# The first stage of a two-layer hybrid backbone: TensorE's order written by hand, fold weights a step ahead, the context moved behind the latent tokens

## The chip, the cores and the metric

The kernel runs on one NeuronCore of a Trainium2 chip. The core has a matrix engine (TensorE, PE in the profile, with its weight loads as PEld), a vector engine (VectorE, DVE), a scalar engine (ScalarE, ACT), GpSimd (POOL) and a queue that issues the loads and stores (SyncE, SP). They run side by side, each in its own fixed order of instructions, and wait for each other through semaphores. The metric is the time of one execution on the device in microseconds (us). Matrix products read SBUF and write PSUM, which has eight banks of 128 x 512 fp32 numbers.

## The reference

The model has two layers. Layer 0 joins a convolution branch and a gated linear recurrence, layer 1 is a pooling mixer. The work of the stage that is changed comes from these lines (cut):

```python
shift, scale, gate = jnp.split(sc @ mod_w[l] + mod_b[l], 3, axis=-1)      # sc = silu(c), 1024 numbers
hx = modulate(rmsnorm(x, norm_g[l]), shift[:, None], scale[:, None])      # x: 1024 tokens x 1024
shift_c, scale_c, gate_c = jnp.split(scc @ mod_w[l] + mod_b[l], 3, axis=-1)
hc = modulate(rmsnorm(ctx, norm_g[l]), shift_c, scale_c)                  # ctx: 256 tokens x 1024
# layer 0
va, vg, ga, xb, gb = jnp.split(hx @ w_in, ...)        # convolution value, its gate, gate A, recurrence input, gate B
xb_c = hc @ w_in[:, 3 * W_CONV:3 * W_CONV + W_LRU]    # the context gives the recurrence its start
u = va * sigmoid(vg)                                  # then a convolution of 31 taps
u_b = depthwise_conv(xb, sconv_w, sconv_b, (2, 1))    # 4 taps, context and latent tokens
r, i = sigmoid(u_b @ w_r + b_r), sigmoid(u_b @ w_i + b_i)      # per head of 128, both directions
log_a = -8 * r * softplus(-lam)                       # "decay rates"
# layer 1
z = h @ w_in;  d = pool(u) - u;  y = einsum(d, w_grp) * scale
```

Pooling acts along the tokens and the group product along the channels, so layer 1's `w_in` and `w_grp` can be multiplied with each other beforehand. The kernel does that ("fold"): 4 groups, each a product of 1024 x 512 by 512 x 512. The output is the latent stream after both layers and a final RMSNorm, in fp32.

## The kernel before

**Layout.** All matrices lie transposed: 128 channels on the partitions, tokens along the row. `x` is 8 tiles of 128 x 1024, the context 8 pieces of 128 x 256 in two tiles of 128 x 1024. Large products keep fp32 accuracy by splitting each operand into a high part (rounded to fp32r) and a low part (the rest), and adding three products: high x high, high x low, low x high. The split is a cast on ScalarE (`split`, L103) and a subtraction (L104) on VectorE or GpSimd. A product of one weight column block with all 8 tiles is 24 matmuls per 512 tokens (`mm3`, `mm3_fixed`).

**The first stage** (from the start to the last `modulate_ctx`). It does three things interleaved by hand in program order:

- *Folds of groups 0 and 1* (`fold`, a generator that `fold_some(n)` advances). One step (g, kp) loads a weight tile `wu`, splits it, and makes two halves s = 0, 1, each 12 matmuls into one PSUM bank (L260 to L262), a copy by ScalarE (L265) and a store to DRAM (`wfold`, L266). The group's own matrix (`graw`, split to `gh`, `gl`) is loaded once.
- *RMSNorm statistics and modulation of the latent tokens.* `x_load(k)` loads a tile and adds its squares (ScalarE squares, VectorE adds). `rstd_cols` turns the sums into roots: small products `ms_x` (L203, one column each), a square root, a diagonal matrix `dg`, and a product of it with ones that spreads the roots over all partitions (L210). The modulation's rows are made in four blocks b: `mod_loads` loads four tiles `modw` of 512 KB, each multiplied with SiLU of c and c_ctx (`modr`, L326, weights of 32 columns); `mod_cols` turns the rows into columns (`modt`, L335). `modulate(k)` then scales tile k, and splits it into `h0h`, `h0l`. A block serves two tiles.
- *The context*: `ctx_load`, `ctx_scale` (root through `ms_c`, L191), `ctx_split`, into `cth`, `ctl`.

**After it** comes a loop over 8 heads j, with every engine's order written by hand (`on` gives each instruction an edge to the one before it on its engine; L444). Step j makes vg, va, the next head's xb and its context part xbc, and the gate products g (L444 all); VectorE makes the recurrence's short convolution (`uc`), the scans and the long convolution, which `fill(n)` hands out tap by tap. In step 0 the gates of layer 0 (the third part of the modulation, for c alone) are made by VectorE: eight tiles of `modT` in the recurrence's tiles `l`, each multiplied with the spread SiLU(c) (`cL`) and summed.

**What sets the order.** In the first stage loads go through `load` (L113), which chains them on SP's queue; stores of the folds are outside of the chain. TensorE's order there is left to a scheduler that orders instructions by its own timeline. At most eight transfers are outstanding: each waits for the one eight places ahead. A pool hands out a tile only when the readers of the one that held its place are done: the weight pool has two places each for raw, high and low parts, the PSUM pool `pm` four banks, `dpool` 16 tiles, `xpool` 8.

Of the kernel before, what the change touches and what calls it, by code (L numbers as in the profile page):

```python
# [15 lines left out]
P = 128  # L16
S = 1024
C = 256
# [38 lines left out]
def body(ctx, tc, xT, ctxT, cc, ccol, modT, modW, win, gw, wout, wu, grp, wg, wo1, small, edge, ident, outT):  # L57
# [49 lines left out]
    chain = [None]  # L107

    def load(out, src):
        with ExitStack() as lctx:  # L110
            if chain[0] is not None:
                lctx.enter_context(tc.issue_after(chain[0].ins))
            d = nc.sync.dma_start(out, src)  # L113
            if chain[0] is not None:
                chain[0] = d

# [28 lines left out]
    nc.sync.dma_start(sm, small)  # L145
    eg = base.tile([P, 4 * 16], F32, name="eg")
    nc.sync.dma_start(eg, edge)
# [23 lines left out]
    nc.scalar.activation(sa, lam, AF.Abs)  # L171
    nc.scalar.activation(sa, sa, AF.Exp, scale=-1.0)
    nc.vector.tensor_scalar(out=sb, in0=sa, scalar1=2.0, scalar2=None, op0=add)
    nc.vector.reciprocal(sb, sb)
    nc.vector.tensor_tensor(out=sz, in0=sa, in1=sb, op=mult)
    nc.vector.tensor_tensor(out=sb, in0=sz, in1=sz, op=mult)
    nc.vector.memset(sa, 1.0 / 17.0)
    for n in range(7, -1, -1):
        nc.vector.tensor_tensor(out=sa, in0=sa, in1=sb, op=mult)
        nc.vector.tensor_scalar(out=sa, in0=sa, scalar1=1.0 / (2 * n + 1), scalar2=None, op0=add)  # L180
    nc.vector.tensor_tensor(out=sa, in0=sa, in1=sz, op=mult)
    nc.vector.tensor_scalar(out=sb, in0=lam, scalar1=-1.0, scalar2=0.0, op0=mult, op1=ALU.max)
    nc.vector.scalar_tensor_tensor(out=sa, in0=sa, scalar=2.0, in1=sb, op0=mult, op1=add)
    nc.vector.tensor_scalar(out=chalf, in0=sa, scalar1=4.0, scalar2=None, op0=mult)
    nc.vector.tensor_scalar(out=cneg, in0=sa, scalar1=-8.0, scalar2=None, op0=mult)
# [11 lines left out]
    def rstd_cols(acc, name, idD, rpool, wn):  # L197
# [4 lines left out]
        for c in range(nt):  # L202
            nc.tensor.matmul(ps[:, c : c + 1], acc[:, c * P : (c + 1) * P], ones[:, 0:1], start=True, stop=True)  # L203
# [6 lines left out]
        nc.tensor.matmul(root[:, :n], ones, t, start=True, stop=True)  # L210
        return root[:, :n]
# [26 lines left out]
    def fold(g, raw_tile, out_tile, g_tile=None, w_tile=None):  # L238
        g_tile = g_tile or dtile
        gh, gl = [], []  # L240
        for i in range(2):
            raw = raw_tile(f"graw_{g}_{i}")
# [10 lines left out]
        for kp in range(KT // 2):  # L253
            wh, wl = (wload(wu[g, kp], f"wu_{g}_{kp}", nc.vector if g == 0 else nc.gpsimd)
                      if w_tile is None else ws[kp])
# [1513 lines left out]
```

## Time and profile before

| | |
|---|---|
| median of 3 runs | 1305.49 us (1301.07 to 1306.55) |
| the profiled execution, its own time | 1306.04 us |
| its span (first to last instruction) | 1304.0 us |
| TensorE busy in the span | 1267.2 us, 97% |
| VectorE busy | 1132.8 us, 87% |
| ScalarE, GpSimd busy | 646.1 us, 300.2 us |
| moved by DMA | 181.81 MB |

The profile is one execution. A row of the time-ordered view has the start in us, the duration in us, the engine, the line of the kernel, the operation, the tiles written and read, the shapes and a count; in brackets stand the idle time of the engine ahead of it and what ended that. Durations of matmuls include their pipeline's latency, so in a dense run the pace is the difference of two starts. In the view by stretches each engine has its busy time and in brackets the number of its instructions; PEclk is the clock that TensorE was granted, as a share of full speed. The chain of waits has start, duration and line of each piece of the chain that ended last. "SPq" is an issue on SP's queue, not the transfer.

### The profile page before, as it was taken

The page shows a single profiled execution, that of the slowest core. Times are in us where ns is not written, and L with a number is a line of the kernel's source. Part 1 is how long each engine was busy: PE and PEld are TensorE (multiplying, and loading weights), DVE is VectorE, ACT ScalarE, POOL GpSimd, SP SyncE. Part 2 cuts the span into 40 slices and gives each one's busy share as a digit, 9 for nine tenths or more (in the row PEclk, how much of TensorE's full clock was granted, in tenths as well). Part 3 has the DMA queues.
Part 4 walks back from the last instruction along what each step waited for, and adds up shares of the span by engine and source line. Part 5 has one row for each costly group of instructions (what it writes and reads, how often), then busy time and mean ns, then how long its engine had stood idle before and what let it go on. Part 6 is the DMA issues. An engine that isn't in the chain of part 4 may idle for free.

```text
span 1304.0 us, 16066 instructions
## 1 busy us (share of the span) xinstructions
PE 1267.2 (97%) x5780; PEld 1036.4 (79%) x5780; DVE 1132.8 (87%) x1756; ACT 646.1 (50%) x935; POOL 300.2 (23%) x151
## 2 busy tenths in 40 slices
PE   7999999999999999999999999999999999999995
PEld 5687888888888887888887778788888888788784
DVE  6669999999999999978968959999999987977776
ACT  7443666566566633236535346634343434645442
POOL 0212644364535546543210022000000000000002
PEclk9999999999999999999999999999999999999997
DMA  9953111122011233442418566334333334868623
GB/s 360 337 178 112 57 42 64 52 62 69 37 57 57 81 127 124 154 145 89 147 47 287 181 195 178 106 121 154 121 126 101 121 113 137 309 217 281 214 85 129
DMA packets 82865, 181.81 MB, mean 139 GB/s; under 512 B 7777, under 2 KB 27617, under 8 KB 82786
## 3 DMA queue, kind: packets, MB, share of 16 engines
q1 hardware_dynamic: 74338, 176.60, 39.9%
q10 hardware_dynamic: 8448, 4.20, 1.1%
q8 instruction: 45, 0.74, 0.2%
q14 instruction: 34, 0.28, 0.1%
HBM read 136.72 MB, written 44.04 MB: 139 GB/s over the span
## 4 chain that ended last, share of the span: by engine, by line
PE 55%; DVE 29%; DMA 8%; issue 3%; ACT 3%; POOL 1%; SPq 0%; POOLq 0%; ACTq 0%; DVEq 0%
DVE conv L444 7%; PE wob L444 6%; PE vg L444 5%; PE va L444 4%; PE xb L444 4%; DVE l L444 4%; PE g L444 3%; DMA yr_t<-y_t 2%; PE fold L262 2%; PE fold L260 2%; PE fold L261 2%; PE ga L135 2%; PE ga L444 2%; PE ga L134 2%; PE ga L136 2%
## 5 line engine op out<-in xcount | busy, mean ns | idle before, releaser
L444 DVE SCALAR_TENSOR_TENSOR conv<-u,sm,conv 128x505 f32<-128x505 f32 (+6 forms) x224 | 153.5, 745 | 1.0
L1588 POOL TENSOR_TENSOR o<-x,rr 128x256 f32<-128x256 f32 (+1 forms) x9 | 8.0, 925 | 452.6 <-ACT rr L1576 449.6
L444 ACT ACTIVATE l<-g,sm 128x512 f32<-128x512 f32 (+1 forms) x96 | 58.7, 618 | 60.0 <-PE g L444 59.2
L104 POOL TENSOR_TENSOR wl_wu<-wr_wu,wh_wu 128x1024 fp32r<-128x1024 f32 x12 | 28.7, 2390 | 171.5 <-ACT wh_wu L103 128.1
L260 PE MATMUL fold<-gh,wh_wu 128*128 128x512 f32 x128 | 53.2, 416 | 4.9 <-ACT wh_wu L103 4.9
L444 POOL TENSOR_TENSOR l<-l,l 128x1280 f32<-128x1280 f32 x16 | 47.1, 2965 | 25.6 <-ACT l L444 15.1
L444 PE MATMUL wob<-ybl,wh_wob 128*128 128x512 f32 x128 | 50.1, 392 | 2.3 <-POOL ybl L444 2.3
L261 PE MATMUL fold<-gl,wh_wu 128*128 128x512 f32 x128 | 51.7, 404 | 0.0
L262 PE MATMUL fold<-gh,wl_wu 128*128 128x512 f32 x128 | 50.3, 405 | 0.3 <-POOL wl_wu L104 0.3
L444 PE MATMUL gb<-h0h,wl_gb 128*128 128x512 f32 x128 | 49.9, 390 | 0.2 <-POOL wl_gb L444 0.2
L444 PE MATMUL gb<-h0l,wh_gb 128*128 128x512 f32 x128 | 49.8, 389 | 0.0
L444 PE MATMUL wob<-ybh,wh_wob 128*128 128x512 f32 x128 | 49.8, 389 | 0.0
L444 PE MATMUL gb<-h0h,wh_gb 128*128 128x512 f32 x128 | 49.8, 389 | 0.0
L444 PE MATMUL vg<-h0h,wh_vg 128*128 128x512 f32 x128 | 49.8, 389 | 0.0
L444 PE MATMUL vg<-h0l,wh_vg 128*128 128x512 f32 x128 | 49.8, 389 | 0.0
L444 PE MATMUL wob<-ybh,wl_wob 128*128 128x512 f32 x128 | 49.8, 389 | 0.0
L444 PE MATMUL vg<-h0h,wl_vg 128*128 128x512 f32 x128 | 49.8, 389 | 0.0
L444 PE MATMUL va<-h0h,wh_va 128*128 128x512 f32 x128 | 49.8, 389 | 0.0
L444 PE MATMUL va<-h0l,wh_va 128*128 128x512 f32 x128 | 49.8, 389 | 0.0
L444 PE MATMUL va<-h0h,wl_va 128*128 128x512 f32 x128 | 49.8, 389 | 0.0
L444 DVE TENSOR_TENSOR_SCAN l<-l,l 128x256 f32<-128x256 f32 (+1 forms) x32 | 48.7, 1521 | 1.1
L103 ACT CAST wq_g<-wr_g 128x512 fp32r<-128x512 f32 x48 | 28.2, 620 | 40.9 <-DVE wr_g L887 12.9
(593 smaller groups left out, 4291.4 us busy)
## 6 DMA issues: line engine op xcount, KB each, us to landing
wr_wu<-wu SPq DMA_DIRECT2D x16, 512.0 KB, 4.5
modw<-modW SPq DMA_DIRECT2D x16, 512.0 KB, 7.1
x_part<-xp SPq DMA_DIRECT2D x32, 256.0 KB, 2.4
mod<-modT SPq DMA_DIRECT2D x32, 256.0 KB, 3.7
wr_v<-wfold SPq DMA_DIRECT2D x16, 512.0 KB, 3.6
wr_g<-wg SPq DMA_DIRECT2D x16, 512.0 KB, 4.4
wr_wo<-wo SPq DMA_DIRECT2D x16, 512.0 KB, 4.6
yr_t<-y_t SPq DMA_DIRECT2D x16, 512.0 KB, 5.9
```

The costliest lines, as they stand in the source:

```text
L103: return (nc.scalar.copy(hi, src), eng.tensor_tensor(out=lo, in0=src, in1=hi.bitcast(F32), op=sub))
L104: eng.tensor_tensor(out=lo, in0=src, in1=hi.bitcast(F32), op=sub))
L134: nc.tensor.matmul(ps, hi[:, kc], xh[k][:, cols], start=(k == 0), stop=False)
L135: nc.tensor.matmul(ps, hi[:, kc], xl[k][:, cols], start=False, stop=False)
L136: nc.tensor.matmul(ps, lo[:, kc], xh[k][:, cols], start=False, stop=(k == ks - 1))
L260: nc.tensor.matmul(ps, wh[:, kc], gh[i], start=(i == 0), stop=False)
L261: nc.tensor.matmul(ps, wh[:, kc], gl[i], start=False, stop=False)
L262: nc.tensor.matmul(ps, wl[:, kc], gh[i], start=False, stop=(i == 3))
L444: last[eng] = f(*args, **kw)
L1588: nc.gpsimd.tensor_tensor(out=o[:, k - k0], in0=v, in1=rr, op=mult)
```

## The change

- **TensorE's order in the first stage is written by hand**: `mm` gives each of its matmuls an edge to the one before it, in program order. Ten products of ones with ones open it.
- **Folds**: the weight tile of the next step is loaded and split a step ahead (`early`); a fold now stops for other work after each half; the weight of the first step is loaded between the two tiles of the group's matrix. Stores are put in a list and issued by `store_folds(n)`, in the load chain; all eight of group 1 come at the very end.
- **Order of loads**: the fold's tiles first; the tables `ident`, `ccol`, `small` behind the first folds, `edge` at the end. The decay rates are made behind the modulation of tile 1.
- **Modulation**: blocks stand between the folds at other places; the last block's tiles are taken from a pool of four tiles (`ctpool`) that the context's `cth`, `ctl` get afterwards.
- **Context**: its tiles take places of `x` tiles; it is scaled and split behind `modulate(7)`; its product for head 0 stands behind both halves of vg0 in place of ahead of them. The weights of vg0 and va0 are loaded ahead of it.
- **Gates of layer 0**: made in the first stage, behind the context's split, with c spread by a load (`partition_broadcast`) in place of a product.

```diff
     def load(out, src):
         with ExitStack() as lctx:
-            if chain[0] is not None:
+            if chained[0] and chain[0] is not None:
                 lctx.enter_context(tc.issue_after(chain[0].ins))
             d = nc.sync.dma_start(out, src)
-            if chain[0] is not None:
+            if chained[0]:
                 chain[0] = d
+
+    def mm(*args, **kw):
+        with ExitStack() as pctx:
+            if pe[0] is not None:
+                pctx.enter_context(tc.issue_after(pe[0].ins))
+            m = nc.tensor.matmul(*args, **kw)
+            if chained[0]:
+                pe[0] = m
...
-    nc.sync.dma_start(sm, small)
-    nc.sync.dma_start(eg, edge)
...
-    nc.scalar.activation(sa, lam, AF.Abs)
...
+    def decay_rates():
+        nc.scalar.activation(sa, lam, AF.Abs)
...
+        def weight(kp):
+            return wload(wu[g, kp], f"wu_{g}_{kp}", nc.vector if g == 0 or kp == 0 else nc.gpsimd)
+
         for i in range(2):
+            if w_tile is None and i == 1:
+                early = weight(0)
             raw = raw_tile(f"graw_{g}_{i}")
...
+            if w_tile is None and kp + 1 < KT // 2:
+                early = weight(kp + 1)
+                yield
...
-                (nc.sync if g < 2 else nc.scalar).dma_start(dst[:, :, s, :].rearrange("m p c -> p m c"),
-                                    o.rearrange("p (m c) -> p m c", c=P))
-            yield
+                if g < 2:
+                    stores.append((dst, o))
+                    yield
...
+    def store_folds(n):
+        while n and stores:
+            load(*stores.pop(0))
+            n -= 1
+
+    ctpool = tc.alloc_tile_pool(name="ctpool", bufs=4)
...
-        fpool = sctx.enter_context(tc.tile_pool(name="fpool", bufs=6))
-        gpool = sctx.enter_context(tc.tile_pool(name="gpool", bufs=6))
+        fpool = sctx.enter_context(tc.tile_pool(name="fpool", bufs=8))
+        gpool = sctx.enter_context(tc.tile_pool(name="gpool", bufs=7))
...
-                raw = dtile(f"modw_{b}_{q}")
+                raw = dtile(f"modw_{b}_{q}") if b < 3 else ctile(f"modw_{b}_{q}", F32)
...
-        for h in range(2):
-            nc.tensor.matmul(ps[h], ones[:1], cx[0][:1, HALF[h]], start=True, stop=True)
-        for h in range(2):
-            nc.scalar.activation(cL[:, HALF[h]], ps[h], AF.Silu, scale=float(D))
+        warm = psum("warm")
+        for i in range(10):
+            mm(warm[:, :P], ones, ones, start=True, stop=True)
+
+        def spread_c():
+            load(cL, cc[0].partition_broadcast(P))
+            nc.scalar.activation(cL, cL, AF.Silu)
+
+        def gates():
+            for m in range(2 * KT, 3 * KT):
+                raw = xtile(f"mod0_{m}")
+                load(raw, modT[0, m])
+                nc.vector.scalar_tensor_tensor(out=raw, in0=raw, scalar=1.0, in1=cL, op0=mult, op1=mult,
+                                               accum_out=m0[:, 0, m : m + 1])
...
+        fold_some(4)
+        x_load(0)
+        x_load(1)
+        fold_some(3)
+        x_load(2)
+        x_load(3)
+        x_load(4)
+        store_folds(2)
+        fold_some(3)
+        load(idx, ident)
+        load(ccv, ccol)
+        nc.scalar.activation(cpad[:, :, 0:2], ccv, AF.Silu)
+        load(sm, small)
+        store_folds(2)
+        fold_some(3)
+        for k in range(5, 8):
+            x_load(k)
+        store_folds(2)
+        fold_some(3)
+        rx = [rstd_cols(acc[h][:, :H], f"x{h}", idx, spool, h) for h in range(2)]
+        mod_loads(0, range(4))
+        store_folds(2)
+        for _, roots in rx:
+            roots()
+        rx = [r for r, _ in rx]
+        mod_cols(0)
+        modulate(0)
+        with tc.issue_after(modulate(1)[1].ins):
+            decay_rates()
+        mod_loads(1, range(4))
         fold_some(2)
...
+        with tc.issue_after(last_low[0].ins), tc.issue_after(last_low[1].ins):
+            ctx_load(0)
+            ctx_load(1)
+        w_vg0 = wload(win[KT], "vg0", nc.vector)
         ctx_scale()
         ctx_split(0)
-        ctx_split(1)
-        chain[0] = None
+        ctx_low = ctx_split(1)
+        raw_va0 = wpool.tile([P, D], F32, tag="wr", name="wr_va0")
+        load(raw_va0, win[0])
+        with tc.issue_after(ctx_low[0].ins), tc.issue_after(ctx_low[1].ins):
+            spread_c()
+            gates()
+        store_folds(8)
+        load(eg, edge)
+        chained[0] = False
...
         xc = psum("xbc0")[:, :C]
-        mm3(xc, w, (ch, cl), slice(0, C))
-        w = wload(win[KT], "vg0", nc.gpsimd)
+        w = w_vg0
         uc = utile("uc0")
-        first_tap(0, xc, uc[:, :C])
-        other_taps(0, xc, uc[:, :C])
...
             all_of(mm3_fixed(vg[1], w, (hh, hl), HALF[1]))
+            if state is None:
+                all_of(mm3_fixed(xc, w_xb0, (ch, cl), slice(0, C)))
+                first_tap(0, xc, uc[:, :C])
+                other_taps(0, xc, uc[:, :C])
...
-            if state is None:
-                for m in range(2 * KT, 3 * KT):
-                    part = L[m % 6][:, :D]
-                    nc.sync.dma_start(part, modT[0, m])
...
```

From the loads of step 1's head on, all engines keep the instructions and the order that they had.

135 lines of the change are left out of this document (65 added, 70 removed).

## The prediction

> **What bounds the kernel now.** I read the page's head first, then the busy time of each engine in stretches that I cut myself, then TensorE's instructions in order of time, the chain of waits between 80 and 125 us, and last the other engines' instructions around it.
>
> ```profile
> span 1304.0 us, 16066 instructions
> ```
> ```profile
> core 0: us, PE busy (x) PEld busy (x) DVE busy (x) ACT busy (x) POOL busy (x), PEclk, DMA share, GB/s
> 0.00:10.29 10.29, 3.75 (x5) 1.16 (x5) 6.42 (x31) 7.33 (x10) 0.20 (x4) 1.00 0.73 260
> 10.29:16.50 6.21, 6.21 (x15) 4.82 (x16) 5.57 (x11) 4.51 (x8) 0.00 (x0) 1.00 1.02 412
> 16.50:29.20 12.70, 12.70 (x57) 10.46 (x56) 7.64 (x12) 8.99 (x16) 0.00 (x0) 1.00 1.03 408
> 29.20:36.60 7.40, 7.40 (x55) 4.14 (x54) 2.97 (x5) 3.46 (x6) 0.00 (x0) 0.77 1.06 389
> ...
> 82.00:120.00 38.00, 36.11 (x184) 30.55 (x182) 29.04 (x39) 11.03 (x14) 8.54 (x4) 1.00 0.47 159
> 120.00:300.00 180.00, 180.00 (x863) 151.80 (x864) 173.37 (x233) 109.75 (x127) 81.23 (x32) 1.00 0.15 50
> ```
> TensorE (PE) is the bound: of the span of 1304.0 us it has its idle time almost all at the start, and 180.00 of 180.00 are busy from 120 us on. There the changed kernel has the same instructions in the same order on every engine, so all that the change can do is to move the moment at which the gate products of the first step (g) begin, 119.97 us now, and the clock at which they run. Before it the stage loses time in four ways: a start at 10.29 us; half pace until 16.50 (6.21/15 = 0.41 us a matmul, against 12.70/57 = 0.22 behind it, though the clock column says 1.00); a granted clock of 0.77 between 29.2 and 36.6, which is 2 x 0.23 x 7.4 = 3.4 us at half speed; and a wait at 119.97. DMA is full until 36.6.
>
> ```profile
> 31.87 1.56 PE L203 MATMUL ms_x<-ones,ssq 128*128 128x1 f32 x12
> 45.85 1.07 PE L326 MATMUL modr<-modw,cpad 128*32 128x256 f32 x16
> 51.52 0.95 PE L335 MATMUL modt<-sm,modrow 128*128 128x2 f32 x8
> 81.12 0.59 PE L191 MATMUL ms_c<-ssqc,ones 128*128 128x256 f32 x2
> 94.88 0.28 PE L135 MATMUL xbc<-ctl,wh_xb 128*128 128x256 f32 x1
> 95.00 0.28 PE L136 MATMUL xbc<-cth,wl_xb 128*128 128x256 f32 x1
> 119.97 0.50 PE L444 MATMUL g<-uh,wh_gw 128*128 128x512 f32 x1 [1.89 <-DVE u L444]
> ```
> Three marks serve below: the second modulation block's row sums are in at 46.92 (45.85 + 1.07), the context's mean square (ms_c) runs at 81.12, g begins at 119.97.
>
> **The change, to the first fold.** Five small loads leave the head of SP's queue, and the fold's weight comes second in place of third.
>
> ```profile
> 0.74 0.40 SPq L145 DMA_DIRECT2D sm<-small  x1
> ...
> 2.90 0.90 SPq L113 DMA_DIRECT2D graw<-grp  x2
> ```
> ```profile
> 6.62 1.04 ACT L103 CAST gh<-graw 128x1024 fp32r<-128x1024 f32 x1 [0.30 <-DMA graw<-grp]
> ...
> 9.19 1.04 ACT L103 CAST wh_wu<-wr_wu 128x1024 fp32r<-128x1024 f32 x1
> ```
> 2.90 - 0.74 = 2.16 us of issuing go, and one landing step of (9.19 - 6.62)/2 = 1.29; the first fold matmul moves from 10.29 to 6.8. Ten warming matmuls stand where TensorE has nothing else: no cost. If they lift the clock, the first 24 fold matmuls (weights trickling in) end at 13.0; if not, as today for some 6 us, at 15.3. The trace can't say, since no such matmuls run there; I take 14.2, the middle. Eight more halves of 12 follow, at 12 x 5.46/24 = 2.73 each (row of 24 matmuls below): folds done at 36.0.
>
> **Through the modulation.** All stores now take their place in the load chain, and the second group's first load stands behind the store of the fourth half. That half ends at 14.2 + 2 x 2.73 = 19.7; its copy takes 0.6 (the 512-wide row below), the issue ahead 0.90/2 = 0.45; so the load is issued at 20.7, when the queue has run dry, and lands 6.62 - 2.90 = 3.7 later, 24.4. (512 KB in 1.29 us is the 406 to 412 GB/s of the full stretches.) Behind it come 14 loads of 512 KB at 1.29 and four stores of half the size at 0.65: the last tile of block 1 lands at 45.1, its product ends at 45.6. That is the new wait: TensorE's order by hand puts block 1 ahead of the next fold, which could have run.
>
> ```profile
> 31.19 1.28 ACT L204 ACT_TABLE_LOAD   x1
> 7.57 0.59 ACT L380 ACTIVATE cL<-c 128x512 f32<-128x512 f32 x1
> 33.02 0.69 DVE L207 TENSOR_TENSOR dg_x<-idx,rc_x 128x512 f32<-128x512 f32 x1
> 34.32 0.69 DVE L207 TENSOR_TENSOR dg_x<-idx,rc_x 128x512 f32<-128x512 f32 x1
> 39.75 1.02 PE L210 MATMUL ms_x<-dg_x,ones 128*128 128x512 f32 x2
> ```
> Beside it runs ScalarE's chain to the roots: behind the last fold a copy (0.59, as the 512-wide pass), a weight cast (1.04), a table load (1.28), root and diagonal 33.02 + 0.69 - 32.47 = 1.24, the second 1.30 later, its product 1.0, modt 0.95: 7.4 us, so 43.4. All of it is TensorE's thin work (ms_x of one column, modr of 32). Now the same kind ran 29.2 to 33.4 (31.87 + 1.56) and cost one half-speed stretch of 3.4 us. Here it fills 36.0 to 45.6, so I charge 0.9 to the products in it and 1.4 to the fold behind it; bounds: nothing, and 3.3 + 2.8 if all of it runs at half. Block 1 ends at 46.5.
>
> The Trainium skill, "TensorE: Matmul & The Clock Gate", Part 1, says that the clock falls to half after an idle window of about 3.4 us and returns after a busy one. The length agrees with 3.4 us from 0.77; but TensorE counts as 7.40 of 7.40 busy there, so the letter of "idle" does not. By that letter nothing between 36 and 46 costs clock, and the sum would be 2.3 us less.
>
> From there to ms_c: six fold halves 16.4, three modt 2.85, two blocks of four tiles at 1.07 a pair 4.3, xb0's 48 matmuls 10.9: 34.4. ms_c = 46.5 + 1.4 + 34.4 = 82.3, with the 0.3 below 82.6, against 81.12: **+1.5**.
>
> ```profile
> 4.81 0.17 DVE L179 TENSOR_TENSOR sa<-sa,sb 128x16 f32<-128x16 f32 x1
> 5.02 0.17 DVE L180 TENSOR_SCALAR sa<-sa 128x16 f32<-128x16 f32 x1
> ...
> 52.97 2.72 DVE L347 SCALAR_TENSOR_TENSOR x<-x,a,ms_x 128x512 f32<-128x512 f32 x4
> 55.61 2.65 DVE L351 SCALAR_TENSOR_TENSOR h0l<-x,m,h0h 128x1024 fp32r<-128x1024 f32 x2
> ```
> The decay rates (26 small VectorE operations, one each 5.02 - 4.81 = 0.21: 5.4 us) leave the start, where VectorE waited for loads, and stand between the modulations of tiles 1 and 2. Their cover is gone there: counted from the end of the first modt, the columns (about 0.5), tiles 0 and 1 (2.7 + 2.65), the rates 5.4, the next columns 0.5 and tiles 2 and 3 (2.7), then ScalarE's pass and copy in its order (1.04 + 0.59) make 16.1 until block 2's modt may start. TensorE comes there after 46.5 - 43.4 = 3.1, the charged 1.4, three fold halves 8.2, a modt 0.95 and a block 2.1: 15.8. So 0.3, and every delay of VectorE would add to it. Of the rest, each has one answer: the two products that spread c (most of the 3.75 us in the first stretch) go from where TensorE waited anyway; vg0's weight is split by VectorE (1.2 us, as a 1024-wide operation) in place of POOL behind xb0's matmuls; va0's raw weight and the row of c are loaded when DMA has room; the small tables come later, but ahead of their readers; more buffers of a pool issue nothing.
>
> **From ms_c to g.** This is VectorE's chain, and it now has the eight gate rows (modT) in it, in the 7.04 us where it waited for the context's product.
>
> ```profile
> 89.09 1.05 ACT L103 CAST cth<-cx 128x1024 fp32r<-128x1024 f32 x1 [0.24 <-DVE cx L358]
> ```
> ```profile
> 89.58 5.46 PE vg L444 x24
> ...
> 106.67 12.45 DVE l L444 x16
> ```
> ```profile
> 98.44 1.52 DVE L444 SCALAR_TENSOR_TENSOR uc<-xbc,sm,uc 128x254 f32<-128x254 f32 x3 [7.04 <-ACT uc L444]
> 99.88 3.91 DVE L444 SCALAR_TENSOR_TENSOR uc<-xb,sm,uc 128x1022 f32<-128x1022 f32 x3
> ...
> 107.73 3.41 DVE L444 SCALAR_TENSOR_TENSOR l<-l,cL 128x1024 f32<-128x1024 f32 x1
> ...
> 113.30 1.22 DVE L444 SCALAR_TENSOR_TENSOR l<-l,cL 128x1024 f32<-128x1024 f32 x1
> ...
> 114.45 1.21 DVE L444 SCALAR_TENSOR_TENSOR l<-l,cL 128x1024 f32<-128x1024 f32 x1
> ```
> ```profile
> 103.88 1.27 ACT L444 CAST uh<-uc 128x1280 fp32r<-128x1280 f32 x1 [1.52 <-DVE uc L444]
> 105.53 1.04 ACT L444 CAST wh_xb<-wr_xb 128x1024 fp32r<-128x1024 f32 x1
> ```
> ```profile
> 100.52 2.40 POOL L444 TENSOR_TENSOR wl_va<-wr_va,wh_va 128x1024 fp32r<-128x1024 f32 x1 [18.01 <-ACT wh_va L444]
> 106.65 3.40 POOL L444 TENSOR_TENSOR wl_xb<-wr_xb,wh_xb 128x1024 fp32r<-128x1024 f32 x1 [3.73 <-ACT wh_xb L444]
> ```
> Counted from ms_c. The context is split as now; ScalarE ends its cast at 90.14 - 81.12 = 9.0. Then, new, a table load 1.3 and SiLU of c (two of the 512-wide passes, 1.1): 11.4. Gates: eight at 114.45 - 113.30 = 1.15 are 9.2; one of them took 3.41 beside POOL's operation, which itself took 3.40 for 2.40, and POOL splits va0's weight there again, so 2.3 more: 22.9. Bounds: 20.6 without, 23.9 if the whole 12.45 recurs; the nearer row is the single 3.41, as one POOL operation of that size falls there, not two. Latent taps 3.9 and context taps 1.5: 28.3. Then ScalarE, whose order is kept: from uh to the end of xb1's cast 105.53 + 1.04 - 103.88 = 2.7: 31.0. POOL splits it, 2.4: 33.4. The context product of step 1 has 24 matmuls at 0.12 (95.00 - 94.88); from its third on it needs that split: g at 36.2. Now it is 119.97 - 81.12 = 38.85.
>
> TensorE meanwhile: vg0 10.9, xbc0 2.9 and va0 10.9 end near 26.4, so it stands for most of 7 us (its 2 matmuls at 31 aside), waiting for taps, cast and split; now it waits 1.89. That costs the clock again: 2.5 us lost on what follows (a stretch of some 5 us at half; bounds 0 and 3.4). Effective 38.7: **-0.15**. The fold's eight late stores also hold ScalarE's uc, whose buffer lies where theirs did; the sixth lands near 17.7 (issues from 10.9 behind two gate loads, 0.65 each), and uc is needed only at 22.9: hidden.
>
> **Sum.** 1306.04 (this execution's own time) + 1.5 - 0.15 = 1307.4, say 1307; its time stands 0.55 above the median of 1305.49. About 0.5%, 6.5 us, is what a measurement can tell from no change.
>
> **The rivals.** (1) The clock stays full throughout. Then folds end at 34.8, loads at 43.9, ms_c at 78.8 (-2.3), g at 36.2 (-2.65): 1301. For it: the long dense runs; against it: 0.77 behind only 4 us of thin work.
> (2) TensorE's own sum decides, the gates fit in VectorE's gap: ms_c 78.8, then 0.45 + 10.9 + 2.9 + 10.9 + 2.9 = 28.0, g at 106.8, 13 us sooner: 1293. For it: VectorE idles 7.04 us there; against it: gates and SiLU need 13.9, and xb1's split stands behind them.
> (3) It ends slower: the clock is at half wherever TensorE isn't dense. Folds end at 37.1, roots and block 1 take 3.3 more, the fold 2.8, so ms_c is at 87.3 (+6.2), and the stall costs 3.4 (+0.75): 1313. It decides from about 6 us of loss above what I charged; the rows of 0.77 and 0.41 speak for it, the dense 2 us of roots against it.
> (4) The warming does nothing and the first folds run as today: +1.1, a part of the forecast's own range, not a case beside it.
>
> **How the numbers follow.** Forecast 0.45 (alone 1303 to 1311), (1) 0.18, (2) 0.13, (3) 0.24. The range leaves out most of (2) and the far end of (3): 1296 to 1316. Faster by over 0.5% (below 1299): (2) and half of (1): 0.22. Slower (above 1312): most of (3): 0.21. Within: 0.57.
>
> **What would show it.** Right: the first fold near 6.8; a stretch without transfers near 20 us; block 1's last tile at 45; PEclk below 1 between 36 and 50; TensorE idle some 7 us ahead of step 1's context product, released by POOL's wl_xb; gates one of which is over 3 us. Wrong: ms_c before 79, or g less than 30 us behind it; or TensorE waiting anywhere behind g.

## The result and the profile after

The changed kernel takes 1314.49 us, the median of 6 runs (1310.86 to 1317.87), against 1305.45 us of the kernel before in the same comparison: a ratio of 1.0072, 95% interval 1.0049 to 1.0094. It is 9 us, or 0.7%, slower. The profiled execution took 1313.92 us, 7.9 more than that of the kernel before.

The page's head, and the busy time of each engine in stretches cut at the marks of TensorE's program: the first fold (6.74), the end of the first group's and two halves of the second group's folds (36.49), the end of modulation block 1 (48.03), the beginning of the wait for the third modt (59.52), the return of the full clock (69.50), ms_c (88.28), and the second gate product (128.18).

```profile
span 1312.0 us, 16081 instructions
```
```profile
core 0: us, PE busy (x) PEld busy (x) DVE busy (x) ACT busy (x) POOL busy (x), PEclk, DMA share, GB/s
6.74:16.50 9.76, 9.23 (x32) 7.21 (x33) 5.66 (x6) 6.68 (x10) 0.00 (x0) 0.83 0.98 378
16.50:36.49 19.99, 19.99 (x89) 16.53 (x89) 12.95 (x18) 16.89 (x28) 0.00 (x0) 1.00 0.98 332
36.49:48.03 11.54, 9.27 (x94) 4.87 (x92) 5.64 (x13) 5.28 (x8) 2.36 (x1) 1.00 1.04 406
48.03:59.52 11.49, 11.49 (x80) 8.43 (x76) 10.71 (x36) 3.50 (x5) 2.37 (x1) 1.00 1.03 408
59.52:69.50 9.98, 7.37 (x46) 4.65 (x47) 8.94 (x13) 6.55 (x9) 2.35 (x1) 0.66 0.58 197
69.50:88.28 18.78, 18.78 (x89) 15.65 (x87) 11.90 (x20) 8.21 (x16) 0.00 (x0) 1.00 0.68 252
88.28:128.18 39.90, 32.63 (x153) 27.29 (x152) 32.74 (x46) 13.75 (x16) 6.55 (x3) 0.91 0.38 114
128.18:421.98 293.80, 293.80 (x1402) 247.43 (x1401) 280.71 (x367) 183.15 (x207) 138.54 (x55) 1.00 0.18 57
```

Behind the first folds (6.74 to 16.50, where the forecast had charged half pace), two stretches have a clock below 1 and an idle TensorE at once, 59.52 to 69.50 and 88.28 to 128.18. Where PEclk is below 1, the time at half speed is twice what it lacks to 1, times the length of the stretch: 2 x 0.34 x 9.98 = 6.8 us in the first. In the second it is 6.8 us too (six full microseconds at 0.50 from 121 to 127, and parts of two). Behind the second gate product nothing is idle, and from there to the first matmul of gb in the last step both kernels need the same time, 293.80 and 293.91. So up to gb all the difference lies in the stage ahead of that product; behind gb both executions took the same time too, 890.0 and 890.1.

TensorE's instructions in order of time, with the idle time ahead of each and what ended it, first the changed kernel's, then two of the kernel before:

```profile
6.74 0.50 PE L123 MATMUL fold<-gh,wh_wu 128*128 128x512 f32 x1 [1.52 <-ACT wh_wu L103]
47.46 0.64 PE L123 MATMUL modr<-modw,cpad 128*32 128x256 f32 x8 [0.64 <-DMA modw<-modW]
62.13 1.46 PE L123 MATMUL modt<-sm,modrow 128*128 128x2 f32 x8 [2.61 <-ACT modrow L370]
77.40 0.39 PE L144 MATMUL xb<-h0h,wh_xb 128*128 128x512 f32 x1
88.28 0.59 PE L201 MATMUL ms_c<-ssqc,ones 128*128 128x256 f32 x2
111.32 0.50 PE L517 MATMUL va<-h0h,wh_va 128*128 128x512 f32 x1 [2.77 <-ACT sg L517]
119.55 0.38 PE L517 MATMUL xbc<-cth,wh_xb 128*128 128x256 f32 x1 [2.46 <-ACT wh_xb L517]
121.98 0.58 PE L517 MATMUL xbc<-cth,wl_xb 128*128 128x256 f32 x1 [1.93 <-POOL wl_xb L517]
126.84 0.41 PE L517 MATMUL g<-uh,wh_gw 128*128 128x256 f32 x1
421.98 0.40 PE L517 MATMUL gb<-h0h,wh_gb 128*128 128x512 f32 x1
```
```profile
77.95 0.39 PE L134 MATMUL xb<-h0h,wh_xb 128*128 128x512 f32 x1
116.86 0.28 PE L444 MATMUL g<-uh,wh_gw 128*128 128x256 f32 x1
413.88 0.40 PE L444 MATMUL gb<-h0h,wh_gb 128*128 128x512 f32 x1
```

The first matmul of xb0 is a better cut than ms_c, because TensorE has the same products behind it in both kernels (ms_c stands 3.2 us into xb0 in the one and at its end in the other). Up to xb0 the change gains 0.55 us (77.40 against 77.95), in spite of a wait of 2.61 us at the third modt and 6.8 / 2 = 3.4 us lost to the clock behind it. From xb0 to gb it loses 344.58 - 335.93 = 8.65 us: waits of 2.77 + 2.46 + 1.93 = 7.16 and 3.4 us of clock, against the single wait of 1.89 before. Together that is 8.1 us, the difference at gb and nearly all of the result.

### The profile page after: what moved, and what is told of

It is laid out like the page before. It is cut to its first block, busy times and chain, and to the rows that moved or that the text cites. A ratio compares the mean times of both kernels' runs of the same rounds, so it can differ in the third digit from the quotient of the medians.

```text
span 1312.0 us, 16081 instructions
## 1 busy us (share of the span) xinstructions
PE 1270.5 (97%) x5796; PEld 1042.3 (79%) x5796; DVE 1138.2 (87%) x1758; ACT 647.9 (49%) x936; POOL 293.2 (22%) x149
## 3 DMA queue, kind: packets, MB, share of 16 engines
q1 hardware_dynamic: 74480, 177.12, 39.9%
## 4 chain that ended last, share of the span: by engine, by line
PE 45%; DVE 33%; DMA 12%; issue 5%; ACT 3%; POOL 1%; SPq 0%; POOLq 0%; DVEq 0%; ACTq 0%
DVE conv L517 6%; PE wob L517 6%; PE vg L517 5%; PE xb L517 4%; PE va L517 4%; DVE l L517 3%; PE fold L123 3%; PE g L517 3%; DVE ws L1376 2%; DMA wr_v<-wfold 2%; PE xbc L517 2%; PE ga L145 2%; PE ga L517 2%; PE ga L144 2%; PE ga L146 2%
```

## The experiments

Times are ratios to the kernel before, measured beside it on the same chip. The marks are those of each run's profiled execution: the start of xb0, of gb in the last step, and the time between them, which holds 334 us of TensorE's work.

| kernel | median, us | ratio (95%) | xb0 | gb | between |
|---|---|---|---|---|---|
| before | 1305.45 | | 77.95 | 413.88 | 335.9 |
| changed | 1314.49 | 1.0072 (1.0049 to 1.0094) | 77.40 | 421.98 | 344.6 |
| changed, again | 1314.20 | 1.0068 (1.0051 to 1.0084) | 77.93 | 422.35 | 344.4 |
| rates moved | 1311.79 | 1.0050 (1.0033 to 1.0067) | 72.14 | 415.65 | 343.5 |
| TensorE kept busy | 1313.11 | 1.0062 (1.0040 to 1.0084) | 75.41 | 419.14 | 343.7 |
| stores early | 1317.04 | 1.0092 (1.0073 to 1.0111) | 75.93 | 419.57 | 343.6 |
| gates split | 1305.07 | 1.0004 (0.9991 to 1.0016) | 74.85 | 411.14 | 336.3 |
| gates back in step 0 | 1306.29 | 1.0015 (1.0003 to 1.0026) | 76.24 | 414.36 | 338.1 |
| rates moved, gates split | 1302.40 | 0.9989 (0.9975 to 1.0002) | 73.62 | 409.90 | 336.3 |
| rates and fold stores moved | 1305.91 | 1.0007 (0.9991 to 1.0023) | 70.72 | 413.34 | 342.6 |
| no warming | 1312.49 | 1.0056 (1.0035 to 1.0077) | 75.83 | 418.12 | 342.3 |
| all edits, no warming | 1298.84 | 0.9952 (0.9937 to 0.9967) | 69.95 | 406.24 | 336.3 |
| and the next head's split early | 1295.14 | 0.9923 (0.9908 to 0.9938) | 69.03 | 403.32 | 334.3 |
| the same with warming | 1296.22 | 0.9940 (0.9921 to 0.9959) | 70.50 | 404.80 | 334.3 |

**The decay rates.** They go from behind tile 1's modulation to the wait for the roots:

```diff
-        with tc.issue_after(modulate(1)[1].ins):
+        modulate(1)
+        with tc.issue_after(last_sum[0].ins):   # the last sum of squares of x
             decay_rates()
```

> The changed kernel with one thing moved: the decay rates' VectorE operations stand behind the last sum of squares, where VectorE waits 4.7 us for the roots, and no longer between the modulations of tiles 1 and 2. Theory A (the rates are what TensorE waits for at the third modt, 2.6 us, and the half clock of 62.8 to 69.4, 3.3 us, is a consequence of that wait): the third modt starts without a wait, the clock stays at 1.00 behind it, ms_c comes 5 to 6 us earlier, at 82 to 83, and the time falls by 5 to 6 us, to about 1308. Rival B (the clock is lost to the thin products themselves, modt and 32 modr): the wait goes, but PEclk is still 0.5 for some 6 us between 60 and 70, and only 2 to 3 us are won, 1311 to 1312. Rival C (something else is late there too, ScalarE's pass over tile 3 or its copy): less than 1 us is won.

The busy times of the engines in the stretch around the third modt, of the changed kernel and then with the rates moved:

```profile
57.00:71.00 14.00, 11.39 (x64) 7.61 (x63) 12.71 (x22) 7.25 (x9) 2.35 (x1) 0.76 0.59 213
```
```profile
57.00:71.00 14.00, 14.00 (x99) 10.98 (x92) 11.22 (x21) 8.15 (x11) 2.37 (x1) 1.00 0.69 254
```

TensorE has no idle time there any more, 14.00 of 14.00, and the clock is 1.00; the third modt runs at 60.15. ms_c runs at 83.02, 5.3 us earlier, as Theory A said, and in the trace B and C fall. The median doesn't bear that out in full: 1311.79 is 2.7 us below that of the changed kernel and not 5 to 6, a time that B had given. The ratio is 1.0050, where gb, 1.8 us behind that of the kernel before, alone gives 1.0014, below the interval; the last section comes back to that.

**Wait or clock.** Ten products that nobody reads fill the wait, into the bank that modt uses next:

```diff
+            if b == 2:
+                for i in range(10):
+                    mm(bank, ones_r, hh[0][:, :H], start=True, stop=True)
             for m in range(2 * KB):
                 mm(pst[:, m], row[:, m * P : (m + 1) * P], col(O_SEL, 2), start=True, stop=True)
```

> The changed kernel with ten products of 128 x 512 that nobody reads (10 x 0.227 = 2.3 us) put in the 2.6 us in which TensorE waits for the third modt. The wait for VectorE stays. Theory A (the idle time brings the half clock): PEclk stays at 1.00 from 60 to 70, ms_c comes 3.3 us earlier, at 85, and the time is 3 us below that of the changed kernel. Rival B (thin products bring it): the third modt starts at 62.1 as before, the clock still falls, and the time is the same within 1 us.

TensorE's instructions in order of time in this run, first the ten products, then the third and the fourth modt:

```profile
60.04 2.46 PE L123 MATMUL modt<-h0h,ones_r 128*128 128x512 f32 x10
62.34 1.05 PE L123 MATMUL modt<-sm,modrow 128*128 128x2 f32 x8
68.85 1.05 PE L123 MATMUL modt<-sm,modrow 128*128 128x2 f32 x8 [0.65 <-ACT modrow L370]
```

The third modt is as late as before (62.34), but the clock stays at 1.00 from 57 to 71, and ms_c comes at 86.38. That is 1.9 us earlier and not 3.3: the fourth modt now waits 0.65 for VectorE's chain, which the slow clock had covered. The time moved by 1.4 us, too little for its interval. This one execution doesn't show that the idle time brings the half clock, as the run with split gates below has a like wait and keeps its clock. All runs together do: of the five profiled executions of kernels with the change in which TensorE stands idle for 1.8 to 2.6 us ahead of the third modt, four have a clock below 1 between 57 and 71 us; of the eight in which it doesn't, with the same thin products at that place, none has.

**The same kernel once more.**

> The changed kernel once more, without an edit, to see how much of its first stage is the same from execution to execution. If the half-clock stretches are fixed by the program: 3.4 us near 8 to 11, 6.8 us from 62 to 69 and 6.8 us from 120 to 127 again, and ms_c at 88 to 88.5. If their number and length depend on where the clock's own window falls: the waits (2.6 us at the third modt; 2.8, 2.5 and 1.9 us between vg0 and g) come again within 0.5 us, while the half-clock time between 50 and 130 is another multiple of about 3.4 us, and ms_c and g differ by up to 3 us. The time is 1311 to 1318 in either case.

The waits were 2.34, 3.09, 2.19 and 1.92 us, the half-clock stretches 3.4, 6.8 and 6.8 us at the same places, ms_c at 88.81. The two executions are alike. But the other kernels with the wait at the third modt show that its price isn't fixed: the stretch from 57 to 71 of the kernel with early stores (a wait of 2.36 us), of that with the gates back in step 0 (1.79), and of that with split gates (2.34):

```profile
57.00:71.00 14.00, 11.64 (x75) 8.20 (x76) 13.04 (x23) 8.54 (x11) 2.35 (x1) 0.88 0.58 212
```
```profile
57.00:71.00 14.00, 12.21 (x90) 8.25 (x83) 13.14 (x23) 8.30 (x11) 2.36 (x1) 0.88 0.65 228
```
```profile
57.00:71.00 14.00, 11.06 (x79) 8.17 (x78) 13.21 (x21) 8.67 (x11) 2.38 (x1) 1.00 0.56 204
```

Half speed lasts 2 x 0.12 x 14 = 3.4 us in the first two, nothing in the third, 6.8 us in the changed kernel, after a wait of about the same length.

**Behind ms_c: the stores.** The eight late stores of the folds go ahead of c's row and the gate rows:

```diff
         load(raw_va0, win[0])
+        store_folds(8)
...
-        store_folds(8)
         load(eg, edge)
```

> The changed kernel with the eight late stores of the second group issued ahead of c's row and the gate rows, in place of behind them. ScalarE's uc, which waited until 108.2 for them, then comes 6 to 7 us earlier, sg with it, and TensorE does not stand 2.8 us in the middle of va0. Theory (VectorE's chain of gates, taps and casts decides when the next head's context product can run): g stays within 1 us of 126.8, the idle time goes to the place ahead of that product, and the time is the same within 1.5 us. Rival (the stores' place costs its 2.8 us, and part of the clock): g comes 2 to 4 us earlier and the time is 1310 to 1312.

TensorE's two waits that are left ahead of the first gate product, in order of time:

```profile
117.65 0.58 PE L517 MATMUL xbc<-cth,wh_xb 128*128 128x256 f32 x1 [5.14 <-ACT wh_xb L517]
120.08 0.58 PE L517 MATMUL xbc<-cth,wl_xb 128*128 128x256 f32 x1 [1.64 <-POOL wl_xb L517]
124.73 0.28 PE L517 MATMUL g<-uh,wh_gw 128*128 128x256 f32 x1
```

The wait in the middle of va0 is gone, and the one ahead of the next head's context product is 5.14 us in place of 2.46. The first gate product runs 124.73 - 86.81 = 37.9 us behind ms_c, where it was 38.6, so behind ms_c the theory holds: the idle time mostly moved, and from xb0 to gb only 0.9 us are won. That g is 2.1 us earlier than 126.8, as the rival said, is for 1.5 us the earlier ms_c, behind a third modt that cost 3.4 us at half speed in place of 6.8. The median, 1317.04, is 2.6 us above that of the changed kernel, where the theory had 1.5 at most and the rival a gain.

**Behind ms_c: the gates.** Five of the eight rows are made before the context's root, and the stores stand ahead of the last three:

```diff
+        with tc.issue_after(last_sum[0].ins), tc.issue_after(last_sq[0].ins):
+            spread_c()
+            gates(0, 5)
-        ctx_scale()
+        with tc.issue_after(last_gate[0].ins):
+            ctx_scale()
         ctx_split(0)
         ctx_low = ctx_split(1)
+        store_folds(8)
...
-            spread_c()
-            gates()
-        store_folds(8)
+            gates(5, KT)
```

> The changed kernel with five of the eight gate rows (and SiLU of c ahead of them) made before the context's root, in the 6 us in which VectorE waits for ms_c (83.5 to 89.5), and the late stores of the folds ahead of the last three rows. The decay rates stay where the change put them. Theory A (from ms_c on the gates in VectorE's chain decide: 11.5 us of it, of which TensorE pays what its own 28 us do not cover): g runs at 118 to 121 in place of 126.8, TensorE's idle time between vg0 and g falls from 7.2 us to under 3, and with the clock kept the time is 6 to 9 us lower, 1306 to 1309. Rival B (the gates were hidden; the head's casts and splits in ScalarE's and GpSimd's order decide): g stays within 2 us of 126.8 and so does the time.

The same rows of this run; between ms_c and g the wait for GpSimd's split is the only one over 0.2 us:

```profile
113.56 0.39 PE L523 MATMUL xbc<-cth,wl_xb 128*128 128x256 f32 x1 [1.74 <-POOL wl_xb L523]
116.30 0.28 PE L523 MATMUL g<-uh,wh_gw 128*128 128x256 f32 x1
```

The first gate product runs at 116.30, sooner than Theory A's 118 to 121. From xb0 to gb it takes 336.3 us, 8.3 less than in the changed kernel, and the time is that of the kernel before. Rival B falls. The edit moves the stores too, but these alone were worth 0.9 us there.

**The gates undone.** They are made in step 0 again, as before the change:

```diff
-            spread_c()
-            gates()
+            spread_c()
...
+            if state is None:
+                for m in range(2 * KT, 3 * KT):
+                    part = L[m % 6][:, :D]
+                    nc.sync.dma_start(part, modT[0, m])
```

> The changed kernel with one part undone: the eight gate rows are loaded and made in step 0 again, behind the head's split of uc and ahead of u, as in the kernel before (c's row and its SiLU stay where the change put them). Theory A (behind ms_c the gates' place in VectorE's chain ahead of the taps decides): the taps start at 98.6 where they started at 111.4, the next head's context product no longer waits, the first gate product runs some 30 us behind ms_c in place of 38.6; the second then waits for u, which stands behind the eight rows (12.5 us as before the change), so it runs 33 to 35 us behind ms_c in place of 39.9, and the time is 4 to 6 us lower, 1308 to 1310. Rival B (the stage between ms_c and g costs the same 39 us wherever the gates stand, as in the kernel before, where it was 38.9): the second gate product 38 to 40 us behind ms_c and the time the same within 2 us.

The first gate product runs at 115.53, 28.4 us behind ms_c, and the second at 116.72, 29.6 behind it, sooner than Theory A's 33 to 35: u holds up only a later one, by 1.40 us. From xb0 to gb: 338.1 us, 6.5 less than with the gates where the change put them. Rival B falls. Of the parts of the change that were tried one by one, moving the gates cost most.

**Both together.** The edits of the rates and of the split gates in one kernel.

> The edits of the two runs before it together: decay rates in the wait for the roots, five gate rows ahead of the context's root. If the two costs are independent, as Theory A has it (one ahead of ms_c, one behind it), the gains add: ms_c at 83, g at 112 to 115, and the time 11 to 14 us below the changed kernel, 1300 to 1303, under the kernel before. If one covers the other, g comes no earlier than 117 and the time stays above 1306.

g at 115.06 and the time at 1302.40 are at the edge of what Theory A gave; ms_c at 84.62 is 1.6 us late. This execution lost its clock elsewhere, from 39.6 to 46.4, over the roots and block 1, as the busy times by stretches show:

```profile
36.85:46.50 9.65, 8.90 (x53) 4.03 (x52) 5.39 (x28) 3.92 (x6) 2.35 (x1) 0.65 1.05 406
46.50:57.00 10.50, 10.38 (x85) 7.45 (x87) 9.03 (x16) 4.21 (x5) 2.40 (x1) 1.00 1.03 408
```

TensorE was idle for 0.75 us in these 9.65, in pieces of at most 0.3; its products there are the thin ones (ms_x of one column, modr of 32).

**Loads.** With the rates moved, the first four stores of the folds go behind the second group's loads:

```diff
         x_load(4)
-        store_folds(2)
...
         load(sm, small)
-        store_folds(2)
...
             x_load(k)
-        store_folds(2)
+        store_folds(6)
```

> The run with the decay rates moved, and in addition the first four stores of the folds issued behind the second group's loads and tiles 5 to 7 of x, in place of ahead of them, so that no load waits for a fold's end. Theory (loads run dry for some us near 10 to 22 us because a store stands ahead of them, and block 1's tiles land late for it): the last tile of block 1 lands 2 to 3 us sooner, TensorE's waits for the modulation's tiles (2 us in all) go, ms_c comes 1.5 to 2.5 us before the 83.0 of the run with the rates alone. Rival (ScalarE's roots and VectorE's modulation decide up to block 2): ms_c within 0.7 us of 83.0.

Between 10 and 20 us it loads 392 GB/s where the changed kernel has 317, block 1 waits for no tile, and ms_c comes at 81.70, 1.3 us ahead of the 83.02 without this edit: between theory and rival.

**Warming.** First alone, then at the end of the work on the version without any wait:

> The changed kernel without the ten warming products at the head (ScalarE's and VectorE's order in the first 35 us is slightly another, copies and squares changing places). If the warming lifts the clock: the first 24 fold matmuls run at half pace for some 6 us as before the change (0.43 apart) in place of 2.8 us, so the folds of the first group end about 1.6 us later, and the time, through ms_c, is 1 to 2 us higher unless the loads of the modulation decide. If the warming does nothing: half pace lasts the same 2.8 us, and the time is the same within 1 us.

> The version of the last run (all edits, and the next head's split early) with the ten warming products put back at the head; nothing else differs in it but small exchanges in ScalarE's and VectorE's order that follow from them. If the products warm the clock for the folds: the half pace behind the first fold is shorter than without them (0.43 from one matmul to the next, for some 3 us there), the first group's folds end up to 1.5 us earlier than 36.2 and the time is 1 us or more below 1295. If they do nothing or are too early (TensorE stands 1 to 1.5 us between them and the first fold): folds end within 0.7 us of 36.2 and the time is the same within 1.5 us.

The first of the two doesn't settle it: without warming the half clock fell on 47 to 54, TensorE came later to the third modt and didn't wait there, and so the marks differ for other reasons. The second does. TensorE's first fold matmuls and the end of the half pace (0.43 us from one start to the next, then 0.23), with the warming and then without:

```profile
6.72 0.51 PE L123 MATMUL fold<-gh,wh_wu 128*128 128x512 f32 x1 [1.75 <-ACT wh_wu L103]
7.07 0.39 PE L123 MATMUL fold<-gl,wh_wu 128*128 128x512 f32 x1
7.99 0.79 PE L123 MATMUL fold<-gh,wl_wu 128*128 128x512 f32 x1 [0.53 <-DVE wl_wu L104]
10.71 0.48 PE L123 MATMUL fold<-gh,wl_wu 128*128 128x512 f32 x1
```
```profile
6.73 0.79 PE L123 MATMUL fold<-gh,wh_wu 128*128 128x512 f32 x1 [6.73 <-ACT wh_wu L103]
7.32 0.63 PE L123 MATMUL fold<-gl,wh_wu 128*128 128x512 f32 x1
7.98 0.80 PE L123 MATMUL fold<-gh,wl_wu 128*128 128x512 f32 x1
10.71 0.47 PE L123 MATMUL fold<-gh,wl_wu 128*128 128x512 f32 x1
```

The warming does lift the clock: the first two fold matmuls take 0.51 and 0.39 us with it and 0.79 and 0.63 without. But the third needs the weight's low part and starts at 7.99 and 7.98, TensorE having stood 0.53 us for it in the one, and it runs at half pace in both. The half pace ends at 10.7 in both; the folds end at 36.23 and 36.19, and the times, 1296.22 and 1295.14, agree within the 1.5 us of the expectation. So the warming wins no time that these runs can show.

**A version faster than both.** All edits without the warming, and then the cast and split of the next head's weight ahead of uc's cast:

> All of these edits together (rates, gate rows, stores), and no warming products. If each of the costs is its own: ms_c at 80.5 to 82, g at 110 to 113, and the time 1296 to 1301, under the kernel before. If the stage is bound elsewhere by then (VectorE's chain of modulations, the loads), ms_c stays at 83 and the time at 1301 to 1304.

```diff
+            name = "gb0" if final else f"xb{j + 1}"
+            if state is None:
+                wnext = raw_split(raw_load(win[3 * KT + j + 1], name), name)
             uh, ul = utile(f"uh{j}", F32R), utile(f"ul{j}", F32R)
             cast(uh, uc)
```

> All edits together as before, and the cast and split of the next head's weight ahead of uc's cast in ScalarE's order, since in the run with all edits TensorE still waits 1.75 us for GpSimd's half of that split. If that split is the last thing late: the wait goes, g comes 1.5 to 2 us earlier than 111.4 and the time is 1296 to 1298. Rival (GpSimd's operation then stands beside VectorE's taps, one of which takes 2 us more, as the gate row beside it did, 3.4 for 1.2): uc, uh and ul come 2 us later, TensorE waits for these in the gate product, and g and the time are the same within 0.7 us or later.

The first of the two ran as its expectation said, with ms_c at 80.95, g at 111.40 and 1298.84 us. Of the second, the busy times from ms_c to the second gate product:

```profile
80.00:109.54 29.54, 29.39 (x153) 25.00 (x152) 27.68 (x39) 12.42 (x15) 6.58 (x3) 1.00 0.46 146
```

TensorE is busy there for 29.39 of 29.54 us, in place of 32.63 of 39.90. The rival's price came only in small (one VectorE operation of 0.15 us took 1.15). The time is 1295.14 us, 0.8% below the kernel before (ratio 0.9923, 0.9908 to 0.9938), and some 19 us below the changed one. Of the 2.9 us by which g came sooner (108.48 after 111.40), 0.95 lie ahead of ms_c.

## Why the prediction was right and where it was wrong

The range, 1296 to 1316, held the result; the single time of 1307 was 7.5 us too low, and "within 0.5%", which had most of the chance, didn't come: it is slower by 0.7%. Rival (3) had 1313, but for a cause that isn't the one found.

*Right: the start.* The first fold ran at 6.74 (6.8), the folds ended at 36.49 (36.0). The middle that stood for the unknown warming came nearer than either end (34.8 and 37.1 for the end of the folds). That is luck: neither case came as told, as the clock was lifted, fell back, and was full again at 11.5.

*Right: VectorE's chain behind ms_c*, step by step. Counted from 88.28, forecast first: the cast of the context 9.0 and 9.0, SiLU 11.4 and 11.4, gates 22.9 and 22.9, taps 28.3 and 28.4, cast of the next weight 31.0 and 31.2, its split 33.4 and 33.6. The rows, of VectorE, ScalarE and GpSimd:

```profile
100.87 3.41 DVE L423 SCALAR_TENSOR_TENSOR mod<-mod,cL 128x1024 f32<-128x1024 f32 x1
109.94 1.21 DVE L423 SCALAR_TENSOR_TENSOR mod<-mod,cL 128x1024 f32<-128x1024 f32 x1
115.22 1.51 DVE L517 SCALAR_TENSOR_TENSOR uc<-xbc,sm,uc 128x254 f32<-128x254 f32 x3
```
```profile
118.46 1.03 ACT L517 CAST wh_xb<-wr_xb 128x1024 fp32r<-128x1024 f32 x1
```
```profile
100.78 2.42 POOL L517 TENSOR_TENSOR wl_va<-wr_va,wh_va 128x1024 fp32r<-128x1024 f32 x1 [35.33 <-ACT wh_va L517]
119.57 2.35 POOL L517 TENSOR_TENSOR wl_xb<-wr_xb,wh_xb 128x1024 fp32r<-128x1024 f32 x1 [16.38 <-ACT wh_xb L517]
```

One gate row took 3.41 beside GpSimd's 2.42, as the forecast had it. Splitting the gates took 8.3 us off the way from xb0 to gb and putting them back 6.5, so the gates' place in this chain is shown as the cause of most of that loss.

*Wrong by one step: "-0.15" from ms_c to g.* The forecast's 36.2 is the first gate product; the 119.97 of the kernel before, which it was held against, is the second. The first ran at 116.86 there. With the three small products of g and three of xb between them (1.06 us at full clock, in the run with split gates) the sum is 36.2 + 1.06 + 2.5 = 39.8 where 38.7 was written, and the second gate product ran 128.18 - 88.28 = 39.9 us behind ms_c. So the sum should have given a loss of 0.9 and not -0.15: a reading mistake, not one of mechanism. The 2.5 us of clock were 3.4.

*Wrong: "So 0.3, and every delay of VectorE would add to it".* This is the step that failed. The wait at the third modt was 2.61 us, and it brought 6.8 us at half clock, 3.4 us lost, where the forecast charged no clock. Of the 2.3 us between the two waits, 1.5 are VectorE's chain: from the end of the first modt (44.53) to the third (62.13) it is 17.6 us and not 16.1. One operation among the rates did that (2.0 us more than its usual 0.18), and the row of GpSimd beside it tells why:

```profile
50.38 0.25 DVE L184 RECIPROCAL sb<-sb 128x16 f32<-128x16 f32 x1
50.67 2.17 DVE L185 TENSOR_TENSOR sz<-sa,sb 128x16 f32<-128x16 f32 x1
52.87 0.18 DVE L186 TENSOR_TENSOR sb<-sz 128x16 f32<-128x16 f32 x1
```
```profile
50.44 2.37 POOL L104 TENSOR_TENSOR wl_wu<-wr_wu,wh_wu 128x1024 fp32r<-128x1024 f32 x1 [9.78 <-ACT wh_wu L103]
```

A product of 16 columns took 2.17 us and ended with GpSimd's operation, at 52.8. With the rates moved, no GpSimd operation runs beside it, and the same instruction took 0.18:

```profile
36.36 0.18 DVE L185 TENSOR_TENSOR sz<-sa,sb 128x16 f32<-128x16 f32 x1
```

In the run with the gates back in step 0 GpSimd's operation began only at 50.98, when this product was done (0.18 us). There the next product of the rates was the long one, 2.36 us, and it too ended with GpSimd's operation, at 53.4. So the length goes with GpSimd's operation and not with the instruction. The forecast charged this collision to the gates and forgot it at the rates. The other 0.8 us of the 2.3 is TensorE, which came 15.0 us after the first modt and not 15.8, as the 1.4 us of clock charged to the next fold weren't lost. The Trainium skill, "SBUF — State Buffer", SBUF: two separate sides, says that VectorE and GpSimd share one pair of ports, which an operation with two inputs in SBUF and one of GpSimd hold against each other for the whole instruction; the trace agrees, with 2.17 us for the product of two tiles and 0.25 for the reciprocal of one just ahead of it.

*Wrong in place: the clock.* 2.3 us were charged between 36 and 50 and none at the third modt; it was the other way round, 1.00 from 36.49 to 59.52. Yet the fold behind block 1 began at 48.03, where the sum with the charge had 46.5 + 1.4 = 47.9: block 1 ended 2.4 us later than the 45.6 that the loads were given, and the two errors cancelled, by luck. By the letter of the Trainium skill, "TensorE: Matmul & The Clock Gate", Part 1, that the clock falls after an idle window, nothing would have been charged here; for the clock that was right in the changed kernel. But it isn't the whole: the kernel before and the run with both edits spent 3.4 and 6.8 us at half speed over thin products, with at most 0.3 us of idle time at once in the second. That is what rival (3) describes. It was rare: the other twelve profiled executions have thin products at that place too, and only the one without warming lost its clock over them (from 47 to 54, with waits of 0.6 us for tiles).

*Right in kind, small in effect: the loads.* Loads did run below their pace (317 GB/s from 10 to 20 us), with no stretch without transfers near 20, but one of 99 GB/s from 16 to 17. Block 1's last tile was late, its product at 47.46 where 45.1 was forecast for the landing. Setting the stores back is worth 1.3 us once the rates are out of the way.

*Wrong but without effect: "hidden" for the stores.* ScalarE's uc waited 7.45 us for them until 108.15, and sg and TensorE behind it for 2.77. It cost little, since VectorE's chain came later still: with early stores nearly the same idle time stood at the next wait, and 0.9 us were won from xb0 to gb.

## What to carry to other kernels

A chain of small operations that leaves a place where its engine waited has to be costed against the exact slack of its new place, and with what runs beside it there: here 6.9 us of work, 2.0 of them a collision, met 15.0 - (17.6 - 6.9) = 4.3 us of slack, and the clock more than doubled the 2.6 us of wait that came of it. When an engine's order is written by hand, put such work where the trace shows that engine idle (35 to 40 us, and ahead of ms_c), in pieces that fit: the same operations in the gaps took the time back to that of the kernel before (a ratio of 0.9989 in place of 1.0072), and with the stores and the next head's split moved too it was 0.8% below it. Hold a forecast mark against the same instruction in both kernels, and cut where the work behind is the same.

## What the runs showed that was not expected

Half speed came in pieces of 3.4 us. Every stretch that the clock column shows below 1 in the first 130 us of the fourteen profiled executions is 3.4 or 6.8 us long: 3.4 near 8 to 11 us, 6.8 and 6.8 later in both executions of the changed kernel, 3.4 in the kernel before. A wait of 1.8 to 2.6 us at the same place cost 0, 3.4 or 6.8 us at half speed in different kernels. The Trainium skill, "TensorE: Matmul & The Clock Gate", Part 1, says that the clock is decided in windows of 3.4 us that run freely, so that the point of a change of clock depends on where in a window the work falls. The multiples agree with it; the two alike executions of the changed kernel don't show the free running. By the measured prices a wait of 2 to 3 us is a risk and not a fixed price. Whether thin products count as idle time stays open: twice the clock was lost over them with hardly any idle time, and most often it was kept.

Warming products that end 1 to 1.8 us ahead of the first fold had it begin at full pace in eight of ten executions (0.50 or 0.51 us in place of 0.79). In each of these eight the clock then fell for 3.4 us between 7 and 13 us, and in the pair above the half pace ended at 10.7 us with them and without them.

Open: behind gb no instruction of the kernels differs, yet from there to the end the profiled executions took 887.7 to 894.9 us (changed kernel 890.0 and 890.2, before 890.1), with the differences in layer 1 from 690 us on. Part of it can be read from the traces. From gb to the last product of 512 columns TensorE is idle for 11.3 to 16.1 us, and in that stretch three executions have pieces of 3.4 us at half speed: one piece with early stores, three with the rates moved and the gates split, two in the last row of the table. What sets these waits isn't shown. A mark also is one execution and a median several: held against the kernel before, median and gb differ by 0.7 to 6.6 us, most with early stores (6.6) and with the rates moved (5.3). So a gain of a few us in the first stage need not show in a median, and the causes above rest on the traces of that stage and on several runs that agree.
